# Layer 0 of a two-layer gMLP and attention backbone: 1/sqrt of the gates, and several low parts, change between VectorE and GpSimd

## The chip, the cores and the metric

The kernel runs on one core of a Trainium2 chip. The core has a matrix engine (TensorE, PE in the profile), a vector engine (VectorE, DVE), an engine for functions of one input (ScalarE, ACT), a general engine (GpSimd, POOL) and one that mostly issues transfers (SyncE, SP). Each engine takes its own instructions strictly in the order of the program, and waits on semaphores for the others. The metric is the device time of one execution in microseconds (us), the median over runs.

## The reference

Two layers over 512 latent and 256 context tokens of width 1024. Each layer:

```
h  = modulate(rmsnorm(x))                      # scale and shift from the condition, by w_mod
z  = h @ w_in                                  # q: 8 heads of 64, k, v: 2 heads, u and g: 512 each
q, k = rope(rmsnorm(q) per head), rope(rmsnorm(k) per head)
attn = softmax(q k^T / 8) v                    # context sees context, latents see all
gm   = gelu(u) * (w_s @ layernorm(gelu(g)) + b_s)   # 4 groups of 128 channels, chunks of 128 positions
x   += gate1 * ([attn, gm] @ w_out)
x   += gate2 * (relu(modulate(rmsnorm(x)) @ w_ff1)^2 @ w_ff2)
```

The layer norm of the gate needs 1/sqrt(variance) for each position and group; rmsnorm of q and k needs it for each position and head. In layer 1 the context takes no part beyond its k and v.

## The kernel before, in words

**Products of two parts.** TensorE multiplies in a rounded 32-bit format. To keep the accuracy, each operand is split in a high part (ACT casts it) and a low part (the operand less its high part, one subtraction on DVE or POOL), and each product is made of three matmuls: high by high, low by high, high by low. So every tensor that goes into a matmul passes ACT for its high part and then DVE or POOL for its low part, before PE can use it. `split(hi, lo, src, eng)` does this at L221 (cast) and L222 (low part). `k`, `A`, `B` and `acc`/`e` are names of such buffers; "raw", "hi", "lo" are a weight and its parts.

**Order of the work.** A `Flow` object carries a virtual clock that advances with each matmul written, a list of deferred pieces of work with due times, and fillers; a table `PAR` of numbers sets the due times and the engine of several steps. A tile scheduler then orders the engines' instructions. In the first layer, the columns of `w_in` are worked through in this order: k and v, the gMLP's inputs u (three tiles), three gate tiles A0 to A2, three banks of q (the "head pairs"), three more gate tiles B0 to B2. The spatial mixing, the attention by blocks of 128 queries, and the product with `w_out` follow, woven into each other.

**The steps that the change touches.**

- `rsqrt(v, n, l)`: 1/sqrt. For a nonzero `l` one power on POOL (L298), else nine small DVE operations (L301 to L311), which begin with an estimate by the bits and refine it twice.
- `stack(t1, nh, which)`: normed q or k heads `t1` (`e` for eight heads-by-chunks of latents, `w` for others) are put side by side as high part (ACT, L722) and low part (L723) in the buffer `k`, of which there is one. PE then transposes it (L735) into PSUM `pt`, and ACT copies it out (L736).
- `sink_g`: for a gate tile `s`, after the gelu (ACT L817, L819; DVE L818, L822), statistics by `bn` (L874, L875), the variance plus epsilon (L877), `rsqrt`, four scalings (L880), and the split of the result (`e`, `acc`) for the mixing matmuls `pt<-ws,...`.
- `mixing`: the mixed gate plus bias times its gain (DVE L905), times gelu(u) in `C` (POOL L910).
- `make_gm`: the products in `C`, four groups, are split for `w_out` into `A` (cast L783, low part L784), 128x768 each.
- attention: row maximum (DVE L999), exponential (ACT L1002), transposes of the weights (PE L1018), their split (ACT L1020, DVE L1021); the attention's output `mix` is split into `B` (L221, L222), on POOL for the outputs listed in `PAR["QP"]`, else on DVE.

PSUM has two buffers of each kind `pa`, `pb`, `pt`.

Of the kernel before, what the change touches and what calls it, by code (L numbers as in the profile page):

```python
# [8 lines left out]
F32 = mybir.dt.float32  # L9
# [3 lines left out]
ALU = mybir.AluOpType  # L13
# [21 lines left out]

PAR = {"KF": 1, "XO": 1, "MS": 3, "KB": 6, "S0": 200.0, "S2": 1.0, "BK": 1, "CS": 0, "S1": 2400.0, "NS": 2, "CX": 0,
# [6 lines left out]


def once(fn):

    left = [fn]
    return lambda: left.pop()() if left else None
# [123 lines left out]
def trunk(ctx: ExitStack, tc: tile.TileContext, xT, pk1, pk2, rope, wsT, w_mod, w_tok, w_u, w_out, w_ff1, w_ff2, outT):  # L172
    nc = tc.nc
    vec, act, pe, pool_e = nc.vector, nc.scalar, nc.tensor, nc.gpsimd
# [14 lines left out]
    def unit(tag, shape, dt=F32R):  # L189
        return units.tile(shape, dt, tag=tag, name=nm(tag))  # L190
# [7 lines left out]
    def tk(shape, dt=F32R):  # L198
        return tmp.tile(shape, dt, tag="k", name=nm("k"), bufs=1)
# [4 lines left out]
    def small(n, dt=F32, tag="m", bufs=9):  # L204
        return tmp.tile([128, n], dt, tag=tag, name=nm(tag), bufs=bufs)
# [14 lines left out]
    def split(hi, lo, src, eng=None):  # L220
        act.copy(hi, src)  # L221
        (eng or vec).tensor_tensor(out=lo, in0=src, in1=hi.bitcast(F32), op=ALU.subtract)  # L222
# [71 lines left out]
    def rsqrt(v, n, l=0):  # L294

        if l:
            y = small(n)
            pool_e.tensor_tensor(out=y, in0=v, in1=mhalf[:, 0:n], op=ALU.pow)  # L298
            return y
        yi = small(n, I32)  # L300
        vec.tensor_scalar(yi, v.bitcast(I32), -0.5, 1595932665.0, op0=ALU.mult, op1=ALU.add)  # L301
        y = yi.bitcast(F32)
        t, r = small(n), small(n)
        vec.tensor_tensor(out=t, in0=y, in1=y, op=ALU.mult)
        vec.scalar_tensor_tensor(out=t, in0=t, scalar=-0.703952253, in1=v, op0=ALU.mult, op1=ALU.mult)
        vec.scalar_tensor_tensor(out=y, in0=t, scalar=1.681914091, in1=y, op0=ALU.add, op1=ALU.mult)
        vec.tensor_tensor(out=t, in0=y, in1=y, op=ALU.mult)
        vec.tensor_tensor(out=r, in0=t, in1=v, op=ALU.mult)
        vec.tensor_scalar(t, r, 0.375, -1.25, op0=ALU.mult, op1=ALU.add)
        vec.tensor_tensor(out=t, in0=t, in1=r, op=ALU.mult)  # L310
        vec.scalar_tensor_tensor(out=y, in0=t, scalar=1.875, in1=y, op0=ALU.add, op1=ALU.mult)  # L311
        return y
# [364 lines left out]
    def layer(l, h, nxt, K, kv=None, kv0=0):  # L677
        last = l == DEPTH - 1
        TQ = SEQ if last else T
        NP = TQ // 256  # L680
# [36 lines left out]
            (pool_e if pool or l in PAR['R2'] else vec).tensor_tensor(out=t1, in0=t1, in1=r.rearrange("p (a b) -> p a b", b=nh).unsqueeze(3).broadcast_to([128, 2, nh, 64]), op=ALU.mult)  # L717
            return t1

        def stack(t1, nh, which):  # L720
            stk = tk([128, 2, nh, 192 if which else 128])
            act.copy(stk[:, :, :, 0:64], t1)  # L722
            (pool_e if l in PAR['SK'] else vec).tensor_tensor(out=stk[:, :, :, 64:128], in0=t1, in1=stk[:, :, :, 0:64].bitcast(F32), op=ALU.subtract)  # L723
            if which:
                act.copy(stk[:, :, :, 128:192], t1)
            return stk
# [14 lines left out]
        def turned(t1, nh, which, tp, plan, wait=None):  # L741
            late = []

            @once
            def one():
                stk = stack(t1, nh, which)
                late.append(once(lambda: turn(stk, tp, plan)))
                fl.defer(PAR["TURN%d" % l] if wait is None else 4200.0, late[0])

            def all_of_it():  # L750
                one()
                late[0]()
            turns.append(all_of_it)
            fl.defer(PAR["QK%d" % l] if wait is None else wait, one)
# [22 lines left out]
        def make_gm():  # L777
            for f in mixes:
                f()
            for g in range(4):  # L780
                gm = unit(f"A{g}", [128, 2, T])
                src = U[g // 2][:, g % 2, 0:TQ]
                act.copy(gm[:, 0, 0:TQ], src)  # L783
                (pool_e if g > 1 and not last else vec).tensor_tensor(out=gm[:, 1, 0:TQ], in0=src, in1=gm[:, 0, 0:TQ].bitcast(F32), op=ALU.subtract)  # L784
                GM.append(gm)

        def sink_q(grp):
# [76 lines left out]
        def sink_g(gp):  # L864
            def f(tp, ps):
                v = gelu2(None, ps.rearrange("p t n -> p (t n)"), [128, 512])
                vg, n = [], len(mixes)

                @once
                def rest():  # L870
                    st = small(24, tag="bn", bufs=2).rearrange("p (a b) -> p a b", b=6)
                    mv = small(8, tag="mv", bufs=2).rearrange("p (a b) -> p a b", b=2)
                    for i in range(4):
                        vec.bn_stats(out=st[:, i, :], in_=v[:, i * 128:i * 128 + 128])  # L874
                        vec.bn_aggr(out=mv[:, i, :], in_=st[:, i, :])  # L875
                    ve = small(4)
                    vec.tensor_scalar(ve, mv[:, :, 1], 4 * EPS, None, op0=ALU.add)  # L877
                    r = rsqrt(ve, 4, l)
                    for i in range(4):
                        (pool_e if l in PAR['VG'] else vec).tensor_scalar(v[:, i * 128:i * 128 + 128], v[:, i * 128:i * 128 + 128], mv[:, i, 0:1], r[:, i:i + 1], op0=ALU.subtract, op1=ALU.mult)  # L880
                    if n > 1:
                        mixes[n - 2]()
                    if l:
                        two = unit(("B5", "B6")[n % 2], [128, 2, 512])
                        vg.extend((two[:, 0, :], two[:, 1, :]))
                    else:
                        vg.extend((te(F32R), tmp.tile([128, 512], F32R, tag="acc0", name=nm("acc0"), bufs=1) if n % 2 else te(F32R)))
                    split(*vg, v, pool_e if l in PAR['VL'] else vec)

                @once  # L890
                def mixing():
                    rest()
                    mx = pt((128, 2, 256))
                    for g in range(2):
                        for t in range(2):
                            c = slice(t * 256 + g * 128, t * 256 + g * 128 + 128)
                            w = slice((gp * 2 + g) * 128, (gp * 2 + g) * 128 + 128)
                            for i, (a, b) in enumerate(((0, 0), (0, 1), (1, 0))):
                                mm(mx[:, g, t * 128:t * 128 + 128], vg[a][:, c], ws[:, b, w], i == 0, i == 2, 128)
                    u = U[gp][:, :, tp * 256:tp * 256 + 256]  # L900
                    e = tsm([128, 2, 256])
                    for g in range(2):
                        G_ = gp * 2 + g
                        to = u if G_ == LATE[l] else e
                        vec.scalar_tensor_tensor(out=to[:, g, :].rearrange("p (t q) -> p t q", t=2), in0=mx[:, g, :].rearrange("p (t q) -> p t q", t=2),  # L905
                                                 scalar=gnh[:, G_:G_ + 1], in1=P2("bs")[:, G_ * 128:G_ * 128 + 128].unsqueeze(1).broadcast_to([128, 2, 128]),
                                                 op0=ALU.mult, op1=ALU.add)
                    gs = [g for g in range(2) if gp * 2 + g != LATE[l]]
                    gs = slice(gs[0], gs[-1] + 1)
                    pool_e.tensor_tensor(out=u[:, gs], in0=e[:, gs], in1=u[:, gs], op=ALU.mult)  # L910
                mixes.append(mixing)
                if l == 0 and n == 2 * NP - 1:
                    fl.defer(8000.0, rest)
                    fl.defer(8000.0 + PAR["G0"], mixing)
                else:
                    rest()
                    fl.defer(PAR["G%d" % l], mixing)
            return f
# [420 lines left out]
```

## Time and profile before

| | us |
|---|---|
| runs | 1488.31, 1489.52, 1489.63; median 1489.52 |
| profiled execution | 1489.16 |
| its span in the trace | 1487.3 |
| PE busy | 1449.6 (97%) |
| DVE busy | 887.3 (60%) |
| ACT busy | 636.9 (43%) |
| POOL busy | 355.2 (24%) |
| mean granted PE clock | 0.996 |

The span is the time from the first to the last instruction; what the metric has beyond it lies around the program. A row of a timeline gives the start in us from the span's start, the duration, the engine, the line, the operation, output and inputs by name, the shape, the count of joined instructions, and in brackets how long the engine had been idle before it and which engine and line ended that.

### The profile page before, as it was taken

What the parts mean: (1) busy time and instruction counts of PE and PEld (TensorE: products, weight loads), DVE (VectorE), ACT (ScalarE), POOL (GpSimd) and SP (SyncE); (2) the same over time, 40 slices, a digit from 0 to 9 for tenths busy, and PEclk for the clock granted to TensorE, in tenths of its full rate; (3) what the DMA queues carried; (4) which work ended last, traced back from release to release, by engine and by line L of the source; (5) the groups of instructions that cost most, each with busy time, mean ns of one, the idle gap of its engine ahead of it and who ended that gap; (6) DMA issues with size and microseconds to landing.
All of it is one profiled execution on the core that took longest, in us unless ns stands there. A gap on an engine that the chain in (4) does not pass through costs nothing.

```text
span 1487.3 us, 21983 instructions
## 1 busy us (share of the span) xinstructions
PE 1449.6 (97%) x8626; PEld 1278.7 (86%) x8626; DVE 887.3 (60%) x1605; ACT 636.9 (43%) x1081; POOL 355.2 (24%) x333
## 2 busy tenths in 40 slices
PE   5989999999999999999999999999999999999998
PEld 3889777798889999999989888898889888888887
DVE  5847867787755463444444437767877554444443
ACT  3542445664445452424333234536775323332221
POOL 0432331312054552313232213256122000000000
PEclk9999999999999999999999999999999999999999
DMA  9312534201233333433333311321001332233331
GB/s 371 108 55 74 186 134 150 84 15 49 68 129 114 114 127 114 133 108 117 125 108 124 109 43 58 99 72 58 29 1 57 128 99 91 93 99 99 100 100 57
DMA packets 50088, 148.78 MB, mean 100 GB/s; under 512 B 5440, under 2 KB 6976, under 8 KB 49984
## 3 DMA queue, kind: packets, MB, share of 16 engines
q1 hardware_dynamic: 49408, 146.72, 29.3%
q8 instruction: 68, 1.11, 0.3%
q10 hardware_dynamic: 576, 0.66, 0.1%
q14 instruction: 36, 0.29, 0.1%
HBM read 145.26 MB, written 2.10 MB: 99 GB/s over the span
## 4 chain that ended last, share of the span: by engine, by line
PE 83%; DVE 8%; ACT 3%; POOL 3%; issue 2%; DMA 1%; SPq 0%; POOLq 0%; ACTq 0%; DVEq 0%
PE pa L217 54%; PE pb L217 21%; PE pt L1018 3%; PE pt L217 2%; PE pb L354 2%; POOL m L298 1%; DVE lo L222 1%; DMA A<-in_w_mod 1%; DVE A L522 1%; POOL lo L222 1%; DVE s L880 1%; PE pt L735 0%; ACT hi L221 0%; ACT w L1002 0%; DVE s L526 0%
## 5 line engine op out<-in xcount | busy, mean ns | idle before, releaser
L217 PE MATMUL pa<-A,hi 128*128 128x384 f32 (+2 forms) x1664 | 442.2, 348 | 1.2 <-DVE s L706 0.9
L221 ACT CAST hi<-raw 128x1024 fp32r<-128x1024 f32 x168 | 176.4, 1051 | 447.7 <-PE pa L217 363.0
L222 DVE TENSOR_TENSOR lo<-raw,hi 128x1024 fp32r<-128x1024 f32 x152 | 192.0, 1263 | 231.9 <-ACT hi L221 228.2
L217 PEld LDWEIGHTS pa<-A,hi 128*128 128x128 f32 x1664 | 300.5, 189 | 22.1 <-DVE s L706 1.2
L217 PE MATMUL pa<-A,lo 128*128 128x384 f32 (+2 forms) x832 | 288.6, 347 | 0.0
L217 PE MATMUL pa<-B,hi 128*128 128x512 f32 (+1 forms) x900 | 241.0, 355 | 0.0
L403 POOL TENSOR_TENSOR C<-C,s 128x512 f32<-128x512 f32 x112 | 163.5, 1474 | 310.2 <-ACT s L402 308.9
L217 PEld LDWEIGHTS pa<-B,hi 128*128 128x128 f32 x900 | 159.7, 189 | 24.1
L217 PEld LDWEIGHTS pa<-A,lo 128*128 128x128 f32 x832 | 156.9, 189 | 10.1
L217 PE MATMUL pa<-B,lo 128*128 128x512 f32 (+1 forms) x450 | 159.5, 355 | 0.0
L217 PE MATMUL pb<-B,hi 128*128 128x512 f32 (+1 forms) x600 | 156.9, 350 | 2.0 <-DVE X L954 2.0
L954 DVE SCALAR_TENSOR_TENSOR X<-pa,modT,X 128x512 f32<-128x512 f32 x126 | 79.5, 659 | 129.4 <-PE pa L217 129.4
L954 DVE SCALAR_TENSOR_TENSOR X<-pb,modT,X 128x512 f32<-128x512 f32 (+3 forms) x116 | 70.9, 619 | 80.7 <-PE pb L217 80.4
L217 PE MATMUL pb<-hi,A 128*128 128x256 f32 (+1 forms) x608 | 118.2, 291 | 0.6 <-DVE m L715 0.6
L217 PEld LDWEIGHTS pb<-B,hi 128*128 128x128 f32 x600 | 103.5, 189 | 16.2 <-DVE X L954 3.0
L217 PE MATMUL pb<-B,lo 128*128 128x512 f32 (+1 forms) x300 | 104.2, 347 | 0.0
L217 PEld LDWEIGHTS pb<-hi,A 128*128 128x128 f32 x608 | 97.0, 191 | 2.3 <-PE pb L217 0.8
L402 ACT ACTIVATE s<-k,silu 128x512 f32<-128x512 f32 x112 | 77.2, 715 | 46.7 <-DMA k<-in_w_mod 31.4
L217 PEld LDWEIGHTS pa<-B,lo 128*128 128x128 f32 x450 | 84.9, 189 | 12.0
L217 PE MATMUL pb<-lo,A 128*128 128x256 f32 (+1 forms) x304 | 87.7, 289 | 0.0
L217 PE MATMUL pb<-A,hi 128*128 128x384 f32 (+2 forms) x288 | 80.9, 361 | 1.9 <-POOL A L784 1.0
L1021 DVE TENSOR_TENSOR A<-pt,A 128x384 fp32r<-128x384 f32 (+1 forms) x144 | 73.2, 536 | 9.9 <-ACT A L1020 8.5
(197 smaller groups left out, 2226.7 us busy)
## 6 DMA issues: line engine op xcount, KB each, us to landing
raw<-in_w_ff SPq DMA_DIRECT2D x128, 512.0 KB, 3.5
k<-in_w_mod SPq DMA_DIRECT2D x96, 256.0 KB, 3.0
raw<-in_w_tok SPq DMA_DIRECT2D x16, 512.0 KB, 3.5
raw<-in_w_out SPq DMA_DIRECT2D x16, 512.0 KB, 3.6
lo<-in_w_mod SPq DMA_DIRECT2D x16, 512.0 KB, 4.4
hi<-in_w_mod SPq DMA_DIRECT2D x16, 512.0 KB, 4.1
A<-in_w_mod SPq DMA_DIRECT2D x8, 512.0 KB, 10.0
B<-in_w_mod SPq DMA_DIRECT2D x8, 512.0 KB, 10.2
```

The lines of the kernel that those rows point to most:

```text
L217: pe.matmul(out, a, b, start=start, stop=stop)
L221: act.copy(hi, src)
L222: (eng or vec).tensor_tensor(out=lo, in0=src, in1=hi.bitcast(F32), op=ALU.subtract)
L298: pool_e.tensor_tensor(out=y, in0=v, in1=mhalf[:, 0:n], op=ALU.pow)
L354: pe.matmul(ps[q:q + 32, :], S32[:, k, :], ws_[k2 // 2][:, k2 % 2 * 512:(k2 % 2 + 1) * 512], start=k < ns, stop=k >= KT - ns)
L402: act.activation(p, w, AF.Copy, scale=s)
L403: pool_e.tensor_tensor(out=a, in0=a, in1=p, op=ALU.add)
L522: (pool_e if k % 2 < PAR['LP'].get('%d%d%d' % (l, w, off // 256), 0) else vec).scalar_tensor_tensor(out=h[k][:, 1, off:off + n], in0=t, sc ...
L880: (pool_e if l in PAR['VG'] else vec).tensor_scalar(v[:, i * 128:i * 128 + 128], v[:, i * 128:i * 128 + 128], mv[:, i, 0:1], r[:, i:i + 1] ...
L954: vec.scalar_tensor_tensor(out=xs, in0=src[:, s - off:e - off], scalar=modT[l][:, i * 8 + m, cond:cond + 1], in1=xs, op0=ALU.mult, op1=ALU ...
L1018: pe.transpose(tp_[:, (kt - k0) * 128:(kt - k0) * 128 + 128], p[:, kt * 128:kt * 128 + 128], ident)
L1021: vec.tensor_tensor(out=ptl[:, k0:k0 + step, d], in0=src, in1=pth[:, k0:k0 + step, d].bitcast(F32), op=ALU.subtract)
```

## The change

All of it is in layer 0.

1. `rsqrt` of the six gate tiles runs as one POOL power (128x4) in place of nine DVE operations.
2. The low part of the stacked latent q pairs (eight heads by chunks, 128x512), three in number, moves from POOL to DVE.
3. The low part of twelve attention outputs (128x256) moves from DVE to POOL (`QP` now holds 0 too).
4. The low parts of the gated products change sides: groups 0 and 1 from DVE to POOL, 2 and 3 from POOL to DVE.
5. The low part of the last gate tile moves from POOL to DVE.

```diff
-       "QP": [1], "R1": [1], "R2": [1], "SK": [0], "VG": [], "VL": [0], "LP": {}, "SQ": 0, "CL": 0, "MQ": 0,
+       "QP": [0, 1], "R1": [1], "R2": [1], "SK": [0], "VG": [], "VL": [0], "LP": {}, "SQ": 0, "CL": 0, "MQ": 0,
...
-        def stack(t1, nh, which):
+        def stack(t1, nh, which, dve=False):
             stk = tk([128, 2, nh, 192 if which else 128])
             act.copy(stk[:, :, :, 0:64], t1)
-            (pool_e if l in PAR['SK'] else vec).tensor_tensor(out=stk[:, :, :, 64:128], in0=t1, in1=stk[:, :, :, 0:64].bitcast(F32), op=ALU.subtract)
+            (pool_e if l in PAR['SK'] and not dve else vec).tensor_tensor(out=stk[:, :, :, 64:128], in0=t1, in1=stk[:, :, :, 0:64].bitcast(F32), op=ALU.subtract)
...
-                stk = stack(t1, nh, which)
+                stk = stack(t1, nh, which, wait is not None and nh == 4)
...
                 act.copy(gm[:, 0, 0:TQ], src)
-                (pool_e if g > 1 and not last else vec).tensor_tensor(out=gm[:, 1, 0:TQ], in0=src, in1=gm[:, 0, 0:TQ].bitcast(F32), op=ALU.subtract)
+                (pool_e if g < 2 and not last else vec).tensor_tensor(out=gm[:, 1, 0:TQ], in0=src, in1=gm[:, 0, 0:TQ].bitcast(F32), op=ALU.subtract)
...
-                    r = rsqrt(ve, 4, l)
+                    r = rsqrt(ve, 4, 1)
...
-                    split(*vg, v, pool_e if l in PAR['VL'] else vec)
+                    split(*vg, v, pool_e if l in PAR['VL'] and n < 2 * NP - 1 else vec)
```

The engines' orders differ only within layer 0's attention and what precedes it; SP's order is the same throughout, and PE has the same matmuls in another order. Three places:

PE at the transposes of the first stacked head pair (`k_779`); `pb_1023` is the first gate tile, `hi_682`/`lo_742` are weights. The rows with + stand there in the new order only.

```order
 L217 MATMUL pb_1023<-hi_741,A_46_179 128x256
+L217 MATMUL pb_1023<-lo_742,A_46_179 128x256
+L217 MATMUL pb_1023<-hi_741,A_46_179 128x256
+L217 MATMUL pb_1023<-hi_741,A_47_180 128x256
+L217 MATMUL pb_1023<-lo_742,A_47_180 128x256
+L217 MATMUL pb_1023<-hi_741,A_47_180 128x256
+L217 MATMUL pb_1023<-hi_741,A_48_181 128x256
+L217 MATMUL pb_1023<-lo_742,A_48_181 128x256
 L735 MATMUL pt_830<-c_70,k_779 128x128 x4
```

Seven matmuls of the gate tile now come ahead of the transposes, taken from between later transposes.

DVE at the same place; `s_782` and `s_842` are gMLP inputs in their gelu, `lo_815` is the low part of a weight.

```order
 L818 SCALAR_TENSOR_TENSOR s_782<-s_782,pa_754 128x384
 L222 TENSOR_TENSOR lo_815<-raw_812,hi_814 128x1024
+L723 TENSOR_TENSOR k_779<-e_572,k_779 128x8x64
 L822 SCALAR_TENSOR_TENSOR C_100_482<-s_782,pa_754 128x384
 L818 SCALAR_TENSOR_TENSOR s_842<-s_842,pa_787 128x384
```

The stack's low part enters DVE's order behind the weight's low part.

DVE around the first attention row maximum (L999 on `pa`), before; `s_1753` and `s_1851` are the fifth and sixth gate tile, `A_398` and `A_399` the split products 0 and 1.

```order
L877 TENSOR_SCALAR m_1768<-mv_1759 128x4
L301 TENSOR_SCALAR m_1770<-m_1768 128x4
L304 TENSOR_TENSOR m_1772<-m_1770 128x4
L305 SCALAR_TENSOR_TENSOR m_1772<-m_1772,m_1768 128x4
L784 TENSOR_TENSOR A_398_2161<-C_100_482,A_398_2161 128x768
L306 SCALAR_TENSOR_TENSOR m_1770<-m_1772,m_1770 128x4
L784 TENSOR_TENSOR A_399_2164<-C_100_482,A_399_2164 128x768
L307 TENSOR_TENSOR m_1772<-m_1770 128x4
L308 TENSOR_TENSOR m_1773<-m_1772,m_1768 128x4
L999 TENSOR_REDUCE m_1859<-pa_1856 128x1
```

And after, with the same tiles under other numbers (`s_1713`, `s_1801`):

```order
L877 TENSOR_SCALAR m_1728<-mv_1719 128x4
L880 TENSOR_SCALAR s_1713<-s_1713,mv_1719,m_1730 128x128 x4
L999 TENSOR_REDUCE m_1809<-pa_1806 128x1
L818 SCALAR_TENSOR_TENSOR s_1801<-s_1801,pb_1740 128x512
L1004 RECIPROCAL m_1814<-m_1812 128x1
```

The nine operations of `rsqrt` and the two low parts have left; the four scalings of the fifth gate tile, which stood behind the maximum, now stand ahead of it.

POOL from there on, after; `mhalf` is the exponent of the power, `A_386` and `A_387` the split products 0 and 1, `e_1737` the low part of the fifth gate tile, `m_1983` the sixth tile's.

```order
L298 TENSOR_TENSOR m_1730<-m_1728,mhalf 128x4
L784 TENSOR_TENSOR A_386_2101<-C_100_482,A_386_2101 128x768
L784 TENSOR_TENSOR A_387_2104<-C_100_482,A_387_2104 128x768
L222 TENSOR_TENSOR e_1737<-s_1713,e_1736 128x512
L1007 COPY rc_1816<-m_1814 128x64
L910 TENSOR_TENSOR C_101_483<-s_1836,C_101_483 128x2x256
L222 TENSOR_TENSOR lo_1880<-raw_1877,hi_1879 128x1024
L1007 COPY rc_1869<-m_1867 128x64
L222 TENSOR_TENSOR lo_1913<-raw_1910,hi_1912 128x1024
L1007 COPY rc_1816<-m_1896 128x64
L1007 COPY rc_1869<-m_1931 128x64
L298 TENSOR_TENSOR m_1983<-m_1981,mhalf 128x4
```

The two powers and the two products are new on POOL; the products stand directly behind the power that the scalings wait for.

ACT around the same exponential, after; `e_1736` is the high part of the fifth gate tile, and before it stood behind the exponential (L1002) and L819.

```order
L783 CAST A_386_2101<-C_100_482 128x768
L783 CAST A_387_2104<-C_100_482 128x768
L221 CAST e_1736<-s_1713 128x512
L817 ACTIVATE s_1801<-pb_1740 128x512
L1002 ACTIVATE w_1811,m_1812<-pa_1806,m_1809 128x256
```

The cast of the scaled gate tile now comes ahead of the gelu step and the exponential.

## The prediction

> **What bounds the kernel now.** I read the page first, then PE's waits, then the clock by windows, then each engine around each wait.
>
> ```profile
> span 1487.3 us, 21983 instructions
> PE 1449.6 (97%) x8626; PEld 1278.7 (86%) x8626; DVE 887.3 (60%) x1605; ACT 636.9 (43%) x1081; POOL 355.2 (24%) x333
> ```
>
> PE is busy for 97% of the span. The change adds or removes no matmul, so only two things can move the time: gaps in which PE waits, and stretches at half clock. All edits lie in layer 0 between about 60 and 345 us. These are PE's waits from 60 to 205 us (total, times, longest), and five windows (start:end, length, PE, PEld, DVE, ACT, POOL, clock, DMA share, GB/s):
>
> ```profile
> PE pt L735 <- POOL k L723: 3.4, 2, 2.6
> PE pt L217 <- POOL acc L222: 1.6, 1, 1.6
> PE pt L1018 <- ACT w L1002: 1.5, 1, 1.5
> PE pb L217 <- POOL A L784: 1.0, 2, 0.6
> PE pb L217 <- DVE m L715: 0.6, 1, 0.6
> ```
> ```profile
> 87.00:90.00 3.00, 3.00 (x13) 3.00 (x12) 0.56 (x1) 2.16 (x5) 0.74 (x1) 0.51 0.00 0
> 173.00:176.00 3.00, 3.00 (x14) 1.11 (x12) 2.94 (x10) 1.55 (x4) 1.29 (x2) 0.53 1.02 404
> 193.00:196.00 3.00, 3.00 (x21) 2.54 (x20) 2.29 (x5) 0.45 (x2) 1.27 (x1) 0.50 0.16 63
> 205.00:345.00 140.00, 137.06 (x966) 115.31 (x965) 106.11 (x237) 85.14 (x195) 25.23 (x50) 1.00 0.24 84
> 375.00:1487.30 1112.30, 1102.68 (x6313) 988.73 (x6311) 615.60 (x925) 452.00 (x698) 258.61 (x216) 1.00 0.28 92
> ```
>
> The edits touch four of these waits, and the three longest gaps (2.6, 1.5, 1.6) are each followed by 3 us at half clock: a gap there costs its length and about 1.5 us more (3.0 us at 0.51 are 1.5 us of work). From 205 to 345 us PE misses only 140.0 - 137.1 = 2.9 us. After 375 us nothing is touched.
>
> **Part 1: the low parts of early head pairs, POOL to DVE.** The first stack:
>
> ```profile
> 82.17 0.40 PE L217 MATMUL pb<-hi,A 128*128 128x256 f32 x2
> 83.24 0.40 PE L217 MATMUL pb<-hi,A 128*128 128x256 f32 x2
> 86.28 1.24 PE L735 MATMUL pt<-c,k 128*128 128x128 f32 x8 [2.64 <-POOL k L723]
> 104.48 1.10 PE L735 MATMUL pt<-c,k 128*128 128x128 f32 x8 [0.73 <-POOL k L723]
> ```
> ```profile
> 82.25 1.64 POOL L298 TENSOR_TENSOR m<-m,mhalf 128x8 f32<-128x8 f32 x1
> 83.96 1.04 POOL L717 TENSOR_TENSOR e<-e,m 128x512 f32<-128x512 f32 x1
> 84.96 1.26 POOL L723 TENSOR_TENSOR k<-e,k 128x512 fp32r<-128x512 f32 x1
> ```
> ```profile
> 82.60 1.23 DVE L222 TENSOR_TENSOR lo<-raw,hi 128x1024 fp32r<-128x1024 f32 x1 [0.79 <-ACT hi L221]
> 953.99 0.69 DVE L222 TENSOR_TENSOR B<-s,B 128x512 fp32r<-128x512 f32 x1
> ```
>
> The low part stands on POOL behind a power (1.64) and a product (1.04) of the next heads, so it ends at 86.22. On DVE it stands behind the weight's low part, free at 83.83, and takes 0.69 as the same shape does at 953.99: done at about 84.5. PE gets seven pb matmuls ahead of the transposes (0.12 each: nine begin between 82.17 and 83.24), so it arrives at 83.64 + 0.83 = 84.5. The wait of 2.64 becomes 0 to 0.2, and the half clock behind it goes: -2.5 - 1.5 = -4.0. DVE's next gelu steps are 0.7 later; the ones that PE needs next come after PE's own matmuls. Bounds: if POOL's product gets ahead, DVE's low part ends 1.0 later and the gap is about 1.2: -1.4 without the clock; nothing beyond -4.2 can be won.
>
> Second stack: 0.73 of wait against a low part that is 1.26 - 0.69 = 0.6 shorter, with one 0.17 matmul more ahead: -0.7. Third: the seven matmuls now missing between transposes cost PE 0.83 us of cover; DVE's shorter operation returns 0.6: +0.2. Together **-4.5** (bounds -4.9 and -1.5).
>
> **Part 2: 1/sqrt of the gates on POOL.** Rows of the first gate tile, and of the same chain in layer 1, which uses POOL already:
>
> ```profile
> 118.39 0.17 DVE L877 TENSOR_SCALAR m<-mv 128x4 f32<-128x4 f32 x1
> 120.60 0.60 DVE L880 TENSOR_SCALAR s<-s,mv,m 128x128 f32<-128x128 f32 x2
> 977.55 0.17 DVE L877 TENSOR_SCALAR m<-mv 128x4 f32<-128x4 f32 x1
> 977.80 1.01 POOL L298 TENSOR_TENSOR m<-m,mhalf 128x4 f32<-128x4 f32 x1 [2.16 <-DVE m L877]
> 978.84 0.35 DVE L880 TENSOR_SCALAR s<-s,mv,m 128x128 f32<-128x128 f32 x1 [1.12 <-POOL m L298]
> ```
>
> From L877 to L880 it is 2.21 us by nine DVE operations and 1.29 by POOL: 0.9 earlier for each of six tiles, and 54 DVE operations of some 0.17 less. No wait of PE in the list ends with L311 or L880, so for the early tiles I take 0: PE's own matmuls hide the chain. If POOL's power came late by 1 us, the gate chain would be as before. The 0.6 wait on L715 is of the query norm and stays.
>
> **Part 3: the gated products' low parts, at 165 to 176 us.** This is where I expect a loss.
>
> ```profile
> 167.71 1.58 ACT L783 CAST A<-C 128x768 fp32r<-128x768 f32 x2
> 169.56 0.95 DVE L784 TENSOR_TENSOR A<-C,A 128x768 fp32r<-128x768 f32 x1
> 171.64 0.42 DVE L999 TENSOR_REDUCE m<-pa 128x1 f32<-128x256 f32 x1
> 172.09 0.47 ACT L1002 ACTIVATE w<-pa,m 128x256 f32<-128x256 f32 x1 [2.31 <-DVE m L999]
> 172.71 0.69 PE L1018 MATMUL pt<-c,w 128*128 128x128 f32 x2 [1.48 <-ACT w L1002]
> 196.83 3.61 POOL L784 TENSOR_TENSOR A<-C,A 128x768 fp32r<-128x768 f32 x2 [1.32 <-ACT A L783]
> ```
>
> PE waits 1.48 us for the first exponential, which waits for the row maximum L999 behind two low parts (0.95 each) on DVE. These leave, but the maximum then stands behind L880 x4, and POOL starts two products of 1.81 each at the moment that its power releases L880. What that does to L880 is seen elsewhere:
>
> ```profile
> 184.67 0.60 DVE L880 TENSOR_SCALAR s<-s,mv,m 128x128 f32<-128x128 f32 x2
> 186.64 1.12 DVE L880 TENSOR_SCALAR s<-s,mv,m 128x128 f32<-128x128 f32 x2
> 186.14 1.27 POOL L910 TENSOR_TENSOR C<-s,C 128x512 f32<-128x512 f32 x1 [3.39 <-DVE s L905]
> ```
>
> Two L880 take 0.60 alone and 1.12 beside a POOL product, ending 0.35 after it: the second one stood still until POOL was done. Worked along the new order on PE's old clock: L877 at 168.2 (DVE is some 0.7 ahead), power to 169.4, then L880 and POOL's two products in turn, L880 done at 169.4 + 3.62 + 1.12 = 174.2 instead of 170.5. ACT's order now has the cast of that tile (0.62) and a gelu step (0.61) ahead of the exponential: 174.2 + 1.2 + 0.47 = 175.9 for PE, against 172.71. That is **+3.2**; the half clock follows either gap. Bounds: if L880 isn't held, the maximum comes at 170.5 and ACT at 172.3, -0.4; if a gap of 1.0 also spares the clock, -2.0:
>
> ```profile
> 267.03 0.55 PE L1018 MATMUL pt<-c,w 128*128 128x128 f32 x3 [1.11 <-DVE A L1021]
> ```
>
> **Part 4: the last gate tile, and products 2 and 3.**
>
> ```profile
> 188.15 2.38 POOL L222 TENSOR_TENSOR lo<-raw,hi 128x1024 fp32r<-128x1024 f32 x1
> 190.50 1.26 POOL L222 TENSOR_TENSOR acc<-s,e 128x512 fp32r<-128x512 f32 x1
> L222 POOL TENSOR_TENSOR B<-mix,B 128x256 fp32r<-128x256 f32 x8 | 5.9, 734 | 12.4 <-ACT B L221 12.3
> 344.96 0.42 DVE L222 TENSOR_TENSOR B<-mix,B 128x256 fp32r<-128x256 f32 x1
> ```
>
> The last tile's low part stands behind a weight's (2.38); on DVE it takes 0.69 and doesn't queue. Its gap of 1.6 and the half clock at 193 (1.5), and 0.2 at its edges, go: **-3.3** (bounds -3.3 and 0, if DVE is still full). Then products 2 and 3: 0.95 on DVE for 1.81 on POOL, which alone would take the two waits (1.0) away. But POOL's order puts a low part of the attention output (0.73) ahead of the product L910 that feeds them, and PE has about 2.8 us of work from the mixing to them (an estimate: the 19 matmuls that the new order shows there at 0.12 to 0.17 each), for 0.9 (L905) + 0.7 + 1.3 (L910) + 0.8 (cast) + 0.95 = 4.65 less what overlaps. I work out waits of 1.4, 0.9 and 0.6 us, so +1.8 against the 1.0 of before (bounds -1.0 and +3.3, the latter with a half clock of 1.5). Eleven other output low parts cost POOL 0.73 for DVE's 0.42 with nobody waiting; the last, at 344.96, ends a chain: +0.3. DVE's relief of 12 x 0.42 = 5 us can shorten at most the 2.9 us that PE misses there: -0.5.
>
> [...]
>
> **Sum.** -4.5 + 0 + 3.2 - 3.3 + 1.8 + 0.3 - 0.5 = -3.0. Against the profiled execution's own 1489.16 (1487.3 span and 1.9 around it) that is 1486.2; the median of the runs is 0.36 above that execution, and against it I forecast **1486.4**.
>
> **Rivals.**
> - *No hold at L880.* For it: POOL's power and DVE's low part at 82 us ran side by side, 1.23 as usual. Against it: 186.64. Then -0.4 to -2.0 stands for +3.2: net -6.6 to -8.2, 1481.3 to 1483. With half of the hold, 1484.5. Chance 0.22.
> - *Slower: the hold at L880 grows into a gap chain.* Everything in softmax follows that first maximum; if the 3.2 us return as a second gap with a half clock in Part 4 (+1.5) and the last gate's -3.3 is not realised because DVE, behind by the same 3 us, runs its low part late, the net is -4.5 + 3.2 + 1.8 + 1.5 - 0.2 = +1.8, so 1491.3, and up to +4 if the later gaps also stretch. It decides from the point where DVE is over 2 us late at 190 us. For it: DVE is 2.94 of 3.00 busy at 173 to 176. Against it: 54 operations leave DVE. Chance 0.20, of which 0.09 over the 0.2% line.
> - *The early waits don't go* (POOL's product gets ahead of DVE's low part in Part 1): the net is 0 to +1, 1489.5 to 1490.5. Against it: DVE is free 0.13 us before POOL. Chance 0.08.
>
> **How the numbers follow.** The forecast case (-1 to -4.5) has 0.50. 0.2% or 3.0 us, about what a measurement of this kernel tells from no change, puts the borders at 1486.5 and 1492.5, so the forecast lies on the upper edge of faster. From its case 0.25 is faster, with 0.21 from the rival without a hold: 0.46; slower are 0.09 of the gap chain and 0.02 of the early waits: 0.11; the rest is 0.43. The range leaves out the ends of both outer cases: 1482.0 to 1491.0; the likeliest case alone is 1485.0 to 1488.5.
>
> **What the profile after would show.** Right: no wait above 0.3 on L723 and clock 1.00 near 87; L880 beside POOL's L784 taking 3 us or more around 170, a PE gap on L1002 near 4.7 there; no wait on acc; small gaps on A from L784 or on L910 near 195. Wrong: L880 x4 of 1.1 beside L784 (then it is 4 us better), a clock below 1 near 88, or a new long wait after 205 us.

## The result, and the profile after

The changed kernel takes 1483.62 us (median, 1480.62 to 1484.61) where the kernel before, run beside it, takes 1488.31: a ratio of 0.9966, 95% interval 0.9954 to 0.9978, 4.7 us less. The forecast was 3.0 us less than its own base. In the pair of profiled executions the span falls by 5.8 us, from 1487.3 to 1481.5. Of the eleven executions of experiment e10 below, one took 1780.06 us at a mean granted clock of 0.75, and it is left out of that experiment's ratio and of the median given there (1486.39 with it).

The page after, span and busy times:

```profile
span 1481.5 us, 21923 instructions
PE 1446.6 (98%) x8626; PEld 1275.9 (86%) x8626; DVE 879.6 (59%) x1543; ACT 635.9 (43%) x1081; POOL 363.5 (25%) x347
```

POOL took on 8 us and PE is still the bound. Of PE's waits from 60 to 205 us, after (total, times, longest), these bear on the argument:

```profile
PE pt L1018 <- ACT w L1002: 4.1, 2, 3.9
PE pb L217 <- ACT A L783: 0.9, 1, 0.9
PE pt L735 <- DVE k L723: 0.9, 1, 0.9
PE pt L367 <- DVE s L905: 0.8, 1, 0.8
PE pb L217 <- DVE A L784: 0.6, 1, 0.6
```

The 2.6 us on the stack are 0.9 us now, the 1.6 us on `acc` are gone, and the wait for the first exponential has grown from 1.5 to 3.9 us. The wait on L905, the step that makes the mixed gate, is new. The same stretches by windows (clock is the third column from the end):

```profile
84.00:92.00 8.00, 7.14 (x48) 6.94 (x48) 3.60 (x6) 3.79 (x9) 2.22 (x3) 1.00 0.21 66
171.00:177.00 6.00, 5.13 (x24) 1.77 (x24) 4.94 (x18) 3.57 (x9) 2.89 (x4) 0.72 0.52 213
190.00:197.00 7.00, 5.32 (x41) 4.24 (x41) 5.94 (x13) 4.19 (x11) 2.37 (x4) 1.00 0.58 215
205.00:345.00 140.00, 138.17 (x969) 116.64 (x968) 103.88 (x233) 86.04 (x195) 33.33 (x61) 1.00 0.23 83
```

Of the three stretches at half clock only the one behind the first exponential is left (0.72 over 171 to 177 us, 1.00 in the other windows), and from 205 to 345 us PE misses 1.8 us instead of 2.9. To see where the time went, the same piece of work is found in both traces. Before:

```profile
77.20 0.62 PE L217 MATMUL pa<-A,hi 128*128 128x384 f32 x2 [0.93 <-DVE s L706]
150.34 0.63 PE L735 MATMUL pt<-c,k 128*128 128x128 f32 x4 [0.39 <-DVE m L309]
178.65 0.17 DVE L437 TENSOR_TENSOR modT<-pt,c 128x8 f32<-128x8 f32 x1 [0.30 <-PE pt L367]
229.69 0.17 DVE L437 TENSOR_TENSOR modT<-pt,c 128x8 f32<-128x8 f32 x1
271.38 0.15 DVE L437 TENSOR_TENSOR modT<-pt,c 128x8 f32<-128x8 f32 x1
```

And after:

```profile
78.03 0.61 PE L217 MATMUL pa<-A,hi 128*128 128x384 f32 x2 [0.76 <-DVE s L706]
147.05 0.63 PE L735 MATMUL pt<-c,k 128*128 128x128 f32 x4 [0.38 <-DVE m L309]
177.79 0.17 DVE L437 TENSOR_TENSOR modT<-pt,c 128x8 f32<-128x8 f32 x1 [0.54 <-PE pt L367]
226.59 0.17 DVE L437 TENSOR_TENSOR modT<-pt,c 128x8 f32<-128x8 f32 x1
266.23 0.17 DVE L437 TENSOR_TENSOR modT<-pt,c 128x8 f32<-128x8 f32 x1 [1.63 <-PE pt L367]
```

Differences of differences give the change by stage (the first 77 us, where nothing was edited, happened to run 0.8 us longer): -4.1 up to 150 us, +2.4 at the first exponential, -2.2 up to 230 us, -2.1 up to 271 us, and -0.2 from there to the L488 that PE begins at 370.59 us before and at 365.19 after. Behind that point nothing was edited, and the remaining 1,100 us happened to run 0.4 us shorter.

### The profile page after: what moved, and what is told of

The parts are those of the page before. It is cut to its first block, busy times and chain, and to the rows that moved or that the text cites. A ratio compares the mean times of both kernels' runs of the same rounds, so it can differ in the third digit from the quotient of the medians.

```text
span 1481.5 us, 21923 instructions
## 1 busy us (share of the span) xinstructions
PE 1446.6 (98%) x8626; PEld 1275.9 (86%) x8626; DVE 879.6 (59%) x1543; ACT 635.9 (43%) x1081; POOL 363.5 (25%) x347
## 3 DMA queue, kind: packets, MB, share of 16 engines
q8 instruction: 68, 1.11, 0.3%
## 4 chain that ended last, share of the span: by engine, by line
PE 85%; DVE 7%; ACT 3%; POOL 2%; issue 2%; DMA 1%; SPq 0%; POOLq 0%; ACTq 0%; DVEq 0%
PE pa L217 55%; PE pb L217 22%; PE pt L1018 3%; PE pt L217 2%; PE pb L354 2%; POOL m L298 1%; DVE s L880 1%; POOL lo L222 1%; DVE lo L222 1%; DMA A<-in_w_mod 1%; PE pt L735 1%; ACT hi L221 0%; DVE bn L874 0%; DVE s L822 0%; ACT w L1002 0%
## 5 line engine op out<-in xcount | busy, mean ns | idle before, releaser
L1021 DVE TENSOR_TENSOR A<-pt,A 128x384 fp32r<-128x384 f32 (+1 forms) x144 | 73.1, 535 | 9.9 <-ACT A L1020 8.2
```

The lines of the kernel that those rows point to most:

```text
L1021: vec.tensor_tensor(out=ptl[:, k0:k0 + step, d], in0=src, in1=pth[:, k0:k0 + step, d].bitcast(F32), op=ALU.subtract)
```

## The experiments

The theory to be tested: the gain is that of the early waits and of the wait on `acc`; the products on POOL, which hold VectorE's scalings, cost some 2 us of it. To hold stands for what the rows show: an operation takes longer than its shape does elsewhere, and ends after one of the other engine that began before it (the two scalings at 186.64 us before: 1.12 us for 0.60, ending 0.35 after POOL's product). What makes it longer is not shown. In e1 to e4 the kernel before took 1487.91 us, in e5 to e8 1488.56, in e9 and e10 1487.22, each time run on the same chip.

**e1: the changed kernel, all four products' low parts on DVE.**

```diff
-(pool_e if g < 2 and not last else vec).tensor_tensor(out=gm[:, 1, 0:TQ], ...
+vec.tensor_tensor(out=gm[:, 1, 0:TQ], ...
```

> The changed kernel, but the low parts of all four gated products run on VectorE (two of them ran on GpSimd beside the four scalings L880). [...] Rival (the gap comes from ACT's new order alone, cast and gelu step ahead of the exponential): the gap stays within 0.5 us of 3.9. [...]

Measured: 1479.89 us (1479.49 to 1480.43), ratio 0.9943 (0.9930 to 0.9955), 3.7 below the changed kernel's median. This is the place in the changed kernel, DVE and POOL:

```profile
166.10 4.11 DVE L880 TENSOR_SCALAR s<-s,mv,m 128x128 f32<-128x128 f32 x4 [1.12 <-POOL m L298]
170.13 0.41 DVE L999 TENSOR_REDUCE m<-pa 128x1 f32<-128x256 f32 x1
```
```profile
165.06 1.01 POOL L298 TENSOR_TENSOR m<-m,mhalf 128x4 f32<-128x4 f32 x1 [2.77 <-DVE m L877]
166.03 3.58 POOL L784 TENSOR_TENSOR A<-C,A 128x768 fp32r<-128x768 f32 x2
```

and in e1, DVE, then PE:

```profile
163.92 1.11 DVE L880 TENSOR_SCALAR s<-s,mv,m 128x128 f32<-128x128 f32 x4 [1.12 <-POOL m L298]
164.94 1.82 DVE L784 TENSOR_TENSOR A<-C,A 128x768 fp32r<-128x768 f32 x2
166.68 0.42 DVE L999 TENSOR_REDUCE m<-pa 128x1 f32<-128x256 f32 x1
```
```profile
167.76 0.44 PE L1018 MATMUL pt<-c,w 128*128 128x128 f32 x2 [1.97 <-ACT w L1002]
```

The four scalings take 4.11 us beside POOL's two products (one by one, the first two of them 1.84 each and the others 0.33) and 1.11 without them, with ACT's order the same. The gap is 1.97 us where about 2.0 had been expected, and the half clock stays (0.50 at 170 to 172 us). The hold is shown; ACT's order alone is not the cause. The time fell by 3.7 us where 1.9 had been expected; of the 1.8 more, in the profiled executions 0.85 us is the gap before the first stack, which e1's doesn't have (see e2), and the rest stays open.

**e2: the kernel before with the stack's low parts on DVE alone.**

```diff
-stk = stack(t1, nh, which)
+stk = stack(t1, nh, which, wait is not None and nh == 4)   # low part on vec if so
```

> The kernel before with only the low parts of the early head pairs moved to VectorE. Theory 1 (the changed kernel's gain up to 150 us is this part's): the gap of 2.64 us becomes 0.9 with no half clock behind it, the gap of 0.73 goes, and the time falls by 4.1 us to about 1484.2. Rival (the gain needs the 54 operations less on VectorE too, or is given back at the waits at 171 to 200 us): under 2 us less.

Measured: 1483.55 us (1483.16 to 1484.40), ratio 0.9968 (0.9955 to 0.9980), -4.4 us. The 0.85 us that stay come from a race (which of two engines comes first is decided by a fraction of a microsecond), seen in e2 on DVE and POOL:

```profile
83.02 1.22 DVE L222 TENSOR_TENSOR lo<-raw,hi 128x1024 fp32r<-128x1024 f32 x1 [0.74 <-ACT hi L221]
84.16 1.53 DVE L723 TENSOR_TENSOR k<-e,k 128x512 fp32r<-128x512 f32 x1
```
```profile
83.83 1.31 POOL L717 TENSOR_TENSOR e<-e,m 128x512 f32<-128x512 f32 x1
```

POOL's product begins while DVE still works on the weight, whose low part ends at 84.24, and takes 1.31 us (1.04 in the kernel before); DVE's low part beside it takes 1.53 and ends at 85.69, 0.55 after POOL's. In e1, POOL begins later than DVE's weight ends (83.50 against 83.34), and DVE's low part takes 0.68:

```profile
82.11 1.23 DVE L222 TENSOR_TENSOR lo<-raw,hi 128x1024 fp32r<-128x1024 f32 x1 [0.77 <-ACT hi L221]
83.26 0.68 DVE L723 TENSOR_TENSOR k<-e,k 128x512 fp32r<-128x512 f32 x1
```
```profile
83.50 1.34 POOL L717 TENSOR_TENSOR e<-e,m 128x512 f32<-128x512 f32 x1
```

**e3: the kernel before with only the last gate tile's low part on DVE.**

```diff
-split(*vg, v, pool_e if l in PAR['VL'] else vec)
+split(*vg, v, pool_e if l in PAR['VL'] and n < 2 * NP - 1 else vec)
```

> The kernel before with only the low part of the last gate tile moved to VectorE. Theory 1: the wait of 1.55 us at 190 us goes and the half clock behind it too, the two waits of 0.4 and 0.6 us at 198 stay: 3.0 us less, 1485.3. Rival (VectorE is too late without the power on GpSimd): the wait stays at 1 us or more and the time within 1 us of before.

Measured: 1488.07 us, ratio 1.0003 (0.9994 to 1.0012): nothing. The theory fell, and so does a part of the prediction. DVE, then POOL, in e3:

```profile
187.72 2.31 DVE L222 TENSOR_TENSOR acc<-s,e 128x512 fp32r<-128x512 f32 x1
```
```profile
187.10 2.39 POOL L222 TENSOR_TENSOR lo<-raw,hi 128x1024 fp32r<-128x1024 f32 x1
```

The low part doesn't queue behind the weight's on POOL any more, but is held by it on DVE: 2.31 us for 0.69, ending 0.54 after it.

**e4: the kernel before with only the products' low parts changing sides.**

```diff
-(pool_e if g > 1 and not last else vec)
+(pool_e if g < 2 and not last else vec)
```

> The kernel before with only the low parts of the gated products changing sides. Theory 1 (GpSimd's products hold VectorE's 1/sqrt and scalings): the gap before the first exponential is not shorter than 1.5 us and up to 3 us, the two waits on the products at 198 us shrink by up to 1.0: 0 to 2 us slower, 1488.3 to 1490.3. Rival (the two low parts of 0.95 on VectorE ahead of the maximum were the cause, and taking them away frees it): the gap at 172 us goes below 0.5 with the half clock behind it, 2 to 4 us less.

Measured: 1489.87 us, ratio 1.0014 (1.0005 to 1.0022), 2.0 slower. The gap before the first exponential is 4.91 us, while PE's two waits on products 2 and 3 (0.42 and 0.63 before) are gone: the loss is that of products 0 and 1. On DVE even the small operations of 1/sqrt are held, L877 and L301 take 1.6 and 1.7 us instead of 0.17 beside POOL's two products (3.60 us from 167.81 on):

```profile
168.05 1.62 DVE L877 TENSOR_SCALAR m<-mv 128x4 f32<-128x4 f32 x1
169.71 1.73 DVE L301 TENSOR_SCALAR m<-m 128x4 int32<-128x4 int32 x1
```

**e5: the kernel before with only 1/sqrt on POOL.**

```diff
-r = rsqrt(ve, 4, l)
+r = rsqrt(ve, 4, 1)
```

> The kernel before with only the gates' 1/sqrt as a power on GpSimd. Theory 2 (the power, not the move of the last low part, ends the wait at 190 us: the scaled tile is ready earlier, and the low part stands ahead of the weight's low part on GpSimd): the wait of 1.55 us on acc goes without any other part, the gap before the first exponential grows from 1.5 to about 2.0 since the scalings and both low parts now stand ahead of the maximum, the early gap of 2.6 stays; 1 to 2.5 us less, 1485.4 to 1487. Rival (the power is hidden, and the wait on acc needs the move of the low part): the wait stays, within 1 us of before.

Measured: 1487.74 us, ratio 0.9996 (0.9987 to 1.0005): not told from no change, under the 1 us expected. But the mechanism is there. No wait on `acc` is left, since the tile is ready in time for the low part to come ahead of the weight's on POOL:

```profile
184.43 1.28 POOL L222 TENSOR_TENSOR acc<-s,e 128x512 fp32r<-128x512 f32 x1 [0.43 <-ACT e L221]
185.66 1.28 POOL L910 TENSOR_TENSOR C<-s,C 128x512 f32<-128x512 f32 x1
186.89 2.38 POOL L222 TENSOR_TENSOR lo<-raw,hi 128x1024 fp32r<-128x1024 f32 x1
```

What it wins is given back: PE's waits there are 1.99 before the first exponential (1.48 before), 0.72 before the second, and 1.28 and 0.70 on the products (0.42 and 0.63 before).

**e6: e1 with the last low part back on POOL.** Edit: the diff of e3 undone.

> The kernel of e1 (changed kernel with all products' low parts on VectorE), with the low part of the last gate tile back on GpSimd. Theory 2: it changes nothing there, no wait on acc above 0.3 us, within 0.8 us of e1 (1479.9). Rival: the wait on acc of about 1.5 us comes back, 1.5 to 3 us slower.

Measured: 1478.39 us (1477.89 to 1480.74), ratio 0.9936 (0.9924 to 0.9949), 1.5 us below e1, though the intervals of the two ratios overlap. No wait on `acc` has come back, so in the changed kernel the power ends it. The move of the last low part to DVE wins nothing, and by the waits it costs a little. In the changed kernel it takes 0.69 there, and L905 stands behind it:

```profile
184.80 0.69 DVE L222 TENSOR_TENSOR acc<-s,e 128x512 fp32r<-128x512 f32 x1 [0.61 <-ACT e L221]
185.41 0.87 DVE L905 SCALAR_TENSOR_TENSOR s<-pt,gnh,k 128x256 f32<-128x256 f32 x2
```

In e6 PE's wait on L905 (0.69 in e1) is gone, and its waits at the products, 0.92 and 0.55 in e1, are 0.39 and 0.33.

**e7: e1 with the outputs' low parts back on DVE.**

```diff
-"QP": [0, 1],
+"QP": [1],
```

> The kernel of e1 with the twelve low parts of attention outputs back on VectorE. Prediction's sizes: the product L910 no longer stands behind a low part of 0.73, so the gap of 0.9 before the products shrinks to about 0.3, while the gap of 1.1 us at 267 us comes back: within 0.8 us of e1. Rival (the changed kernel's gain after 205 us, some 2 us by the trace, is these twelve low parts): 1.5 to 2.5 us slower than e1.

Measured: 1482.57 us (1482.06 to 1484.88), ratio 0.9963 (0.9949 to 0.9976), 2.7 us above e1: the rival was right in kind, a little more than it said; a half clock (0.76 at 190 to 197 us) adds to it in the profiled execution. The gap of 1.11 us that stood at 267 us before is back, with its cause in a row of the kernel before that the prediction did not weigh, on DVE and on POOL:

```profile
264.49 2.01 DVE L222 TENSOR_TENSOR B<-mix,B 128x256 fp32r<-128x256 f32 x1
```
```profile
263.85 2.37 POOL L222 TENSOR_TENSOR lo<-raw,hi 128x1024 fp32r<-128x1024 f32 x1 [1.87 <-ACT hi L221]
```

An output's low part, 0.42 us long, is held 1.6 us by a weight's (2.01 us, ending 0.28 after it), and the softmax step L1021 that PE waits for stands behind it.

The other 1 us has no idle row of PE, but PE's order shows it. L354 (products for the modulation, each written to a strip of 32 rows) comes in sets of eight matmuls that run four at a time (two and two begin 0.01 us apart in the rows after, of 0.62 us each). In the kernel before, two of one set stand alone, one after the other, and the remaining six come 2 us later, three at a time; after, the eight are together. Before, then after (the second four begin 0.45 us later):

```profile
234.23 1.04 PE L354 MATMUL pb<-hi,S 128*32 128x512 f32 x2
236.39 0.62 PE L354 MATMUL pb<-hi,S 128*32 128x512 f32 x1
236.39 0.62 PE L354 MATMUL pb<-lo,S 128*32 128x512 f32 x2
```
```profile
231.90 0.62 PE L354 MATMUL pb<-hi,S 128*32 128x512 f32 x2
231.91 0.62 PE L354 MATMUL pb<-lo,S 128*32 128x512 f32 x2
```

The two alone hold PE from 234.23 to 235.21, as long as a whole set (231.90 to 232.89 us after), so the split costs 1.0 us. This set is split in all six kernels with the outputs on DVE (before, e2, e3, e4, e5, e7) and together in all six with the outputs on POOL (after, e1, e6, e8, e9, e10).

**e8: e1 with the products L717 on DVE too, to end the race at 84 us.**

```diff
-(pool_e if pool or l in PAR['R2'] else vec).tensor_tensor(out=t1, in0=t1, in1=r...
+(pool_e if (pool and nh != 4) or l in PAR['R2'] else vec).tensor_tensor(out=t1, in0=t1, in1=r...
```

> The kernel of e1 with the three products e<-e,m (L717) of the early head pairs on VectorE as well, so that GpSimd has nothing of 128x512 beside the stack's low part at 84 us. [...] Rival: VectorE is the bound at 80 us, 1 us slower or more.

Measured: 1484.23 us, ratio 0.9972 (0.9962 to 0.9982), 4.3 us above e1, where 0 to 0.9 us below it had been expected: a miss. The low part takes 0.68, but DVE stands 1.43 us for POOL's power ahead of L717, and the stack behind it; the gap is 2.13 us where e1's profiled execution had none. The profiled execution took 1482.75; what the slower ones lost beyond it is not shown.

```profile
84.59 0.69 DVE L717 TENSOR_TENSOR e<-e,m 128x512 f32<-128x512 f32 x1 [1.43 <-POOL m L298]
85.20 0.55 DVE L818 SCALAR_TENSOR_TENSOR s<-s,pa 128x384 f32<-128x384 f32 x1
85.66 0.68 DVE L723 TENSOR_TENSOR k<-e,k 128x512 fp32r<-128x512 f32 x1
```

**e9: e6 with the low parts of products 0 and 1 waiting for the first maximum.** `minus[0]` is made from that maximum on DVE, times 0 less 1.

```diff
-vec.tensor_tensor(out=gm[:, 1, 0:TQ], in0=src, in1=gm[:, 0, 0:TQ]..., op=ALU.subtract)
+vec.scalar_tensor_tensor(out=gm[:, 1, 0:TQ], in0=gm[:, 0, 0:TQ]..., scalar=minus[0], in1=src, op0=ALU.mult, op1=ALU.add)   # for g < 2; the others as before
```

> The kernel of e6 with the low parts of products 0 and 1 made to wait, on VectorE, for the first row maximum (they are computed as product minus high part by way of a factor of -1 that is derived from that maximum); nothing else in any engine's order moves. Theory (the gap of 1.98 before the first exponential is the two low parts ahead of the maximum, 1.82 us, of which ACT's cast and gelu step hide a part): the gap falls to about 0.9 and, if the half clock behind it goes too, 1.1 to 2.7 us are won: 1475.7 to 1477.3. Rival (the low parts then delay the sixth gate tile, whose statistics now come two transposes later): a wait on the mixing matmuls near 185 us takes it back, within 0.5 us of e6 (1478.4).

Measured: 1477.60 us (1477.02 to 1478.58), ratio 0.9933 (0.9919 to 0.9946), 9.6 us below the kernel before. PE in e9:

```profile
167.22 0.44 PE L1018 MATMUL pt<-c,w 128*128 128x128 f32 x2 [0.93 <-ACT w L1002]
172.18 0.44 PE L1018 MATMUL pt<-c,w 128*128 128x128 f32 x2 [1.02 <-ACT w L1002]
```

The gap is 0.93 as expected, and the half clock went (1.00 from 166 to 176 us), but a second gap, of 1.02, stands at the next exponential. Against e6 the time is 0.8 lower, inside the two intervals. It is the fastest version with e6, and both beat the changed kernel.

**e10: the kernel before with only the outputs' low parts on POOL.** Edit: the diff of e7 the other way, on the kernel before.

> The kernel before with only the twelve low parts of attention outputs moved to GpSimd. Theory (e7: they are worth some 2 us by themselves, of which 1.1 is the gap at 267 us): that gap goes, the products near 200 us wait up to 0.7 more, 1 to 2 us less: 1486.3 to 1487.3. Rival (the prediction's size, +0.3 and -0.5): within 0.5 us of before.

Measured: 1486.09 us, ratio 0.9990 (0.9981 to 0.9999), 1.1 us less, at the edge of what can be told and at the lower end of the 1 to 2 us expected. The gap at 267 us is gone in the trace, and the eight matmuls of L354 are together; the two are 2.1 us, and what takes the rest back is not shown.

## Why the prediction was right, and where not

The time fell as forecast and lies in the range, but 1.4 us below the likeliest case (1485.0 to 1488.5), between the 1483 of the rival without a hold and the 1484.5 of half a hold. That rival's mechanism is refuted, so the number alone would mislead here. Term by term:

- *Early stacks, -4.5:* right. -4.1 in the trace, and alone -4.4 (e2). The bound in the text, POOL's product getting ahead, is what happened in the profiled execution: the gap was 0.85 rather than 0.1 (1.2 had been said). No half clock followed it (1.00 over 84 to 92 us). The 1.5 us for the clock were not certain: e5 and e10 kept a gap of 2.64 and 2.67 us there, and in their profiled executions the clock was 1.00 over 84 to 92 us too.
- *1/sqrt, 0:* wrong in its reason. The sentence "no wait of PE in the list ends with L311 or L880" looked one step too short: the wait on `acc` ends a chain that begins there. The power, not part 5, takes that wait away (e3, e5, e6).
- *Products at the first exponential, +3.2:* right, in the way described: L880 took 4.11 us, 4.74 had been worked out (3.62 + 1.12); PE's gap was 3.9, 4.7 had been said; the stage lost 2.4 us. One reading of the row at 186.64 was off without effect: of the two scalings it was the first that took longer (0.86 and 0.33 us), as here the first two of four (1.84 each).
- *Last tile -3.3 and products 2 and 3 +1.8:* the sum, -1.5, was near the -2.2 measured up to 230 us, but by luck: the price was put on the wrong edit. "On DVE it takes 0.69 and doesn't queue" did not come true in the edit alone: it took 2.31 beside POOL's low part of a weight of 2.39 us (e3). In the changed kernel it did take 0.69, but only because the power made the tile early, and it put a wait of 0.8 on L905 that the sum hadn't. The two waits on the products were 0.9 and 0.6, and one of 0.2 on an exponential followed, where 1.4, 0.9 and 0.6 had been worked out.
- *Outputs on POOL, +0.3 - 0.5:* the term that was mis-sized. From 230 to 271 us it brought 2.1 us. 1.1 of this is the gap at 267, and the other 1.0 is the split set of L354 (e7). The prediction capped this term by the 2.9 us that PE is idle from 205 to 345 us; matmuls that run one or three at a time instead of four are not idle time.
- *Rivals:* "No hold at L880" is refuted by the 4.11 us and by e1. The gap chain did not come about: the delay at the first exponential was not followed by a later half clock (1.00 over 190 to 197 us).

By stages, -4.5, +3.2, -1.5 and -0.2 had been put down, -3.0 in all; the trace has -4.1, +2.4, -2.2 and -2.1, with the last -0.2 a sum of -6.2. The outputs' term is the largest miss (1.9 too small), then the exponential (0.8 too dear) and the last tile (0.7). The 0.8 us that the first 77 us lost and the 0.4 that the end won, where nothing was edited, are in the span's -5.8 but not in this sum, and the medians are 4.7 apart. The median forecast, 1486.4, was 2.8 too high: 1.6 by the size of the gain and 1.2 by its base, the median of three runs, which over seven is 1488.31. Two small sums don't come out: 1489.52 less 3.0 is 1486.5, and the terms of the early stacks give bounds of -4.7 and -1.9 rather than -4.9 and -1.5.

The length of a gap alone did not tell whether a half clock follows. One came after gaps of 3.92 us (changed kernel, 0.72 over 171 to 177 us), 4.91 us (e4, 0.60 there), 1.97 us (e1, 0.50 at 170 to 172 us) and 1.21 us (e3, 0.50 at 193 to 195 us), and none after 2.67 us (e10, 1.00 at 86 to 90 us) or 1.46 and 1.55 us (e2, 1.00 from 164 to 178 and 184 to 197 us). Gaps of nearly one length went both ways: 2.66 us before the first stack in e4 (0.79 over 84 to 92 us) and 2.67 in e10, 1.46 us before the first exponential in e3 (0.72 over 171 to 177 us) and 1.46 in e2. From 60 to 400 us, the stretches at 0.50 begin at 87.08, 172.42 and 192.90 us in the trace of the kernel before and at 171.53 us in that of the changed kernel, and each lasts 3.41 us, 1.7 us of work at that clock. So the same gap may or may not cost that much more; what decides it is not shown, and nothing in these runs varied it on purpose.

## What to carry to other kernels

Before an elementwise operation moves between VectorE and GpSimd, look at what the other engine does in those microseconds. Here a subtraction or product of one engine held subtractions, products and scalings of the other: VectorE's low part of a gate tile took 2.31 us instead of 0.69 beside GpSimd's low part of a weight, without queueing anywhere (e3), its four scalings 4.11 instead of 1.11 beside GpSimd's two products (changed kernel and e1), and GpSimd's product L717 1.31 instead of 1.04 beside VectorE's low part of a weight (e2). Not every row was longer: in the changed kernel two VectorE operations with an input in PSUM, L1021 and L999, took 0.42 and 0.41 us beside GpSimd's low part of a weight at 187.59 us, which took 2.38, and in the kernel before VectorE's low part of a weight took 1.23 us beside GpSimd's power of 1.64, and 1.23 at 126.74 us with GpSimd idle. Look for it in the trace as rows of a known shape that are too long, and ask which operation beside them ends just before they do (0.54 us before in e3, 0.28 in the kernel before at 264.49 us). Where parts of a change interact, price a wait by the whole chain that ends it, not by its last link, and test each part alone: here the move of products 0 and 1 to POOL was a loss inside a gain (e1, e4), and the move of the last tile won nothing (e3, e6).

## What was not expected of the hardware

How long DVE's L723 took changed with a fraction of a microsecond in the starts. In e2 POOL's L717 began at 83.83 us and DVE's L723 0.33 us later, L717 took 1.31 and L723 1.53, and PE's gap before the transposes was 0.85 us. In e1 L723 began at 83.26 us and L717 0.24 us later, L723 took 0.68 and L717 1.34, and PE had no gap there. So some 0.6 us between the starts went with 0.85 us of PE's time. Beside the two products in the changed kernel (3.58 us) the first two scalings took 1.84 us each and the last two 0.33 each, so the longer time was not spread over all four. Beside POOL's power it was otherwise: DVE's low part of a weight took 1.22 us beside one of 1.64 us in e2, and 1.23 in the kernel before. What sets these times is not shown.
